# Start loads, rotation temporaries, pool waits and convolution taps of a hybrid encoder layer, rearranged

## The chip, the cores and the metric

The kernel runs on one core of one Trainium2 chip. What is measured is the time in microseconds that one execution takes on the device; the median of several runs counts. The engines are named as the profile names them: PE (TensorE, matrix products; PEld is its loading of weights), DVE (VectorE), ACT (ScalarE), POOL (GpSimd) and SP (SyncE, which here only issues transfers).

## The reference

One encoder layer is applied to two sequences with the same weights, a prompt of 512 tokens and a sample of 256, width 1024, in 32-bit floats. An attention group and a convolution group work beside each other on the same normed input:

```python
def mixer(h, ...):
    proj = h @ w_in
    cq, ckv, kr, conv_a, conv_g = jnp.split(proj, cut, axis=-1)
    q = (rms_norm(cq, q_norm_g) @ w_uq).reshape(B, S, N_HEADS, QK_NOPE + QK_ROPE)
    kv = (rms_norm(ckv, kv_norm_g) @ w_ukv).reshape(B, S, N_HEADS, QK_NOPE + V_HEAD)
    q_rope, k_rope = apply_rope(q_rope, cos, sin), apply_rope(kr, cos, sin)
    attn = block_attention(qf, kf, v)            # 8 heads, softmax over all tokens
    u = conv_a * jax.nn.sigmoid(conv_g)
    u = depthwise_conv(u, dw_w) + dw_b           # 31 taps, 512 channels, centred
    u = jax.nn.silu(layer_norm(u, conv_ln_g, conv_ln_b))
    merged = jnp.concatenate([rms_norm(attn, attn_out_g), rms_norm(u, conv_out_g)], axis=-1)
    return merged @ w_out

x = x + mixer(rms_norm(x, norm1_g), ...)
x = x + swiglu(rms_norm(x, norm2_g), w_gate, w_up, w_down)   # inner width 2816
return rms_norm(x, final_g)
```

Here `qf` and `kf` are the two parts of each head, 64 numbers without and 32 with rotation, put together; one rotated key part serves all heads.

## The kernel before, in words

Every large product is done in three: an operand is split by `split` into a high part, rounded by ACT (`L107`, with a scale `L110`), and the rest, which DVE subtracts (`L108`), and PE multiplies high by high, high by low and low by high. All products come from `mm` (`L293`). The 768 tokens are 6 blocks of 128; blocks 0 to 3 are the prompt (`s` = 0), 4 and 5 the sample.

The stages follow each other:

- *Convolution's projection.* Four blocks of channels `i`, each over eight slabs `k` of the transposed input `xT`. The slabs come through the load ring `stg`, four buffers with the tag "st", and are split into `hT` with the norm's gain `g1` as the scale. The norm's factor per token comes later: token rows `xr` (two buffers for six rows) are squared and summed by ACT, `build_rb` turns the sums into diagonal matrices `dg` (DVE) and multiplies these with ones on PE (`prb`), which spreads the factors over all partitions (`rb`). `glu(i)` then makes the convolution's input `u`.
- *Latent projections*, `tm_mm` and `tm_tr`, for query and key/value.
- *Query stage*, `q_up`, `v_up`, `k_up`, `kr_up`: heads are unfolded, `rope` rotates a part of each. `q_up` ends with ACT's copy of the block (`L470`) and a rotation of four DVE operations (`L375` to `L378`), whose temporaries `rc` and `rs` come from the pool `cTp`.
- *Attention*, 12 units. A unit transposes queries into `ptq`, splits them into `qh` and `ql`, makes the scores `pss`, takes the maxima `ngmx` (`L711`) and goes on to exponentials and values. Between the units stand the convolution's layer norms (`conv_ln`, which transposes `acc` into `pcl`), its activation, and parts of the output projection, whose results `out_add` adds to `xall` (`L815`). `LN0` is the unit after which the prompt's norm stands.
- *Output projection, SwiGLU feed-forward, final norm.* The feed-forward is by far the longest stage.

The depthwise convolution has no stage of its own. It is 240 instructions on DVE, one for each tap and block of channels (`conv_taps`, `L250`, 120 of 512 columns for the prompt and 120 of 256 for the sample), which are spread over the stages: each `mm` adds its own estimated time, multiplied by the stage's `RATE`, to what is due, and taps are issued until that is paid (`tap_some`). `tap_all` issues what is left ahead of a norm.

The written order isn't the order of execution: a scheduler with costs of its own places the instructions of each engine. `tc.keep_in_program_order` holds an instruction in the order in which it is written; `mm` uses it where `pin` is set.

Memory is taken from pools that are closed and whose place goes to others. With `reuse="pool"`, the default, the first tile of a new pool waits until all that lay in its place is through; with `reuse="tile"` each tile waits only for the tiles that lay where it lies. Ahead of the attention `wkvp`, `tb`, `cTp` and `psA` (the PSUM of all stages so far) are closed and six pools opened.

Of the kernel before, what the change touches and what calls it, by code (L numbers as in the profile page):

```python
# [11 lines left out]
F32 = mybir.dt.float32  # L12
# [5 lines left out]
PSUM = bass.MemoryType.PSUM  # L18

D = 1024  # L20
S0, S1 = 512, 256
T = S0 + S1
NB = T // 128
H, DN, DR, DV = 8, 64, 32, 64
# [11 lines left out]
C_G1, C_QG, C_KG, C_DW, C_DB, C_LG, C_LB, C_OG, C_COS, C_SIN = 0, 8, 11, 13, 137, 141, 145, 149, 157, 253  # L36
# [1 line left out]

RATE = {"A": 0.6, "B": 1.4, "C": 0.6, "D": 1.0, "S": 1.0, "F": 1.2}
SAMPLE_RATE = 0.2

TAPW = 4

LN0 = 4


@with_exitstack
def tile_hybrid_layer(  # L50
# [15 lines left out]
    nc = tc.nc  # L66
    ACT, DVE, POOL, PE = nc.scalar, nc.vector, nc.gpsimd, nc.tensor

    def pool(name, bufs=1, side="left", space=None, reuse="pool"):
        if space is None:  # L70
            cm = tc.tile_pool(name=name, bufs=bufs, side=side, reuse_waits=reuse)
        else:
            cm = tc.tile_pool(name=name, bufs=bufs, space=space, side=side, reuse_waits=reuse)
        es = ExitStack()
        p = es.enter_context(cm)
        return p, es.close
# [3 lines left out]
    stg = ctx.enter_context(tc.tile_pool(name="stg", bufs=4))  # L80
# [6 lines left out]
    def nm(s):  # L87
        uid[0] += 1
        return f"{s}_{uid[0]}"
# [15 lines left out]
    def split(dst_hi, dst_lo, src, scale=None):  # L105
        if scale is None:
            ACT.copy(dst_hi, src)  # L107
            DVE.tensor_sub(dst_lo, src, dst_hi.bitcast(F32))  # L108
        else:
            ACT.activation(dst_hi, src, AF.Copy, scale=scale)  # L110
            DVE.scalar_tensor_tensor(dst_lo, src, scale, dst_hi.bitcast(F32), ALU.mult, ALU.subtract)
# [18 lines left out]
    mhalf = cpool.tile([128, 8], F32, name="mhalf")  # L130
    DVE.memset(mhalf, -0.5)
    g1 = cpool.tile([128, 8], F32, name="g1")
    nc.gpsimd.dma_start(g1, cst[:, C_G1 : C_G1 + 8])
    c = cpool.tile([128, C_N], F32, name="c")
    r1 = cpool.tile([128, NB], F32, name="r1")
    r1sq = cpool.tile([128, NB], F32, name="r1sq")
# [14 lines left out]
    SEQ = ((0, S0), (S0, S1))  # L151
# [20 lines left out]
    cTp, cT_close = pool("cTp")  # L172
# [26 lines left out]
    def conv_chunk(i, j):  # L199
        return wsplit(wab, wconv[i, j], 1024)  # L200

    ss = small.tile([128, NB], F32, tag="ss", name="ss")
    xr = [xrp.tile([128, D], F32, tag="xr", name=nm("xr"), bufs=2) for _ in range(NB)]
# [3 lines left out]
    for k in range(8):  # L207
        if k == 4:
            wc[0, 1] = conv_chunk(0, 1)
        if k < 4:  # L210
            ks = slice(k * 256, (k + 1) * 256)
            t = stg.tile([128, 1024], F32, tag="st", name=nm("st"))
            nc.sync.dma_start(t[:, :256], wconv[0, 0][:, ks])
            split(w0[0][:, ks], w0[1][:, ks], t[:, :256])
        t = stg.tile([128, 1024], F32, tag="st", name=nm("st"))
        (nc.scalar if k == 0 else nc.sync).dma_start(t[:, :T], xT[:, k, :])
        if k == 2:
            nc.sync.dma_start(c, cst)
        for s, (o, n) in enumerate(SEQ):
            split(hT[s][0][:, k, :], hT[s][1][:, k, :], t[:, o : o + n], g1[:, k : k + 1])  # L220

    wc[1, 0] = conv_chunk(1, 0)
    for b in range(NB):
        nc.sync.dma_start(xr[b], xtok[b * 128 : (b + 1) * 128, :])
        ACT.activation(xr[b], xr[b], AF.Square, scale=1.0 / 32.0, accum_out=ss[:, b : b + 1])
        if b == 2:
            wc[1, 1] = conv_chunk(1, 1)
# [50 lines left out]
    def tap_all(s):  # L278
        while True:
            nxt = next_tap(s)  # L280
            if nxt is None:
                return
            nxt[1]()
# [8 lines left out]
    def mm(out, lhsT, rhs, start, stop):  # L292
        pinned(PE.matmul(out, lhsT, rhs, start=start, stop=stop))  # L293
        n = rhs.shape[-1]
        tap_some(n / 2400 * (4 if rhs.dtype == F32 else 1))

    pcs = {}
    pace["rate"] = RATE["A"]

# [19 lines left out]
    for i in range(4):  # L319
        pp = [psA.tile([128, 512], F32, tag="p", name=nm("pc")) for _ in range(3)]  # L320
        ps = [[pp[0], pp[2][:, :256]], [pp[1], pp[2][:, 256:]]]
        for k in range(8):
# [10 lines left out]
            for ag in range(2):  # L333
                o = (k % 4) * 256 + ag * 128
# [10 lines left out]

    pace["rate"] = RATE["B"]

# [17 lines left out]
    def rope(dst, src, b, n, tp):  # L365

        cs = c[:, None, C_COS + b * 16 : C_COS + (b + 1) * 16].to_broadcast([128, 2 * n, 16])
        sn = c[:, None, C_SIN + b * 16 : C_SIN + (b + 1) * 16].to_broadcast([128, 2 * n, 16])
        tcs = tp.tile([128, n, 2, 16], F32, tag=f"rc{n}", name=nm("rc"), bufs=2)
        tsn = tp.tile([128, n, 2, 16], F32, tag=f"rs{n}", name=nm("rs"), bufs=2)  # L370
        s4 = src.rearrange("p n (two f) -> p n two f", two=2)
        d4 = dst.rearrange("p n (two f) -> p n two f", two=2)
        cs4 = cs.rearrange("p (n two) f -> p n two f", two=2)
        sn4 = sn.rearrange("p (n two) f -> p n two f", two=2)
        DVE.tensor_mul(tcs, s4, cs4)  # L375
        DVE.tensor_mul(tsn, s4, sn4)
        DVE.tensor_sub(d4[:, :, 0, :], tcs[:, :, 0, :], tsn[:, :, 1, :])
        DVE.tensor_add(d4[:, :, 1, :], tcs[:, :, 1, :], tsn[:, :, 0, :])  # L378
# [3 lines left out]
    def loc(b):  # L382

        s = b // 4
        return s, slice((b % 4) * 128, (b % 4 + 1) * 128)
# [44 lines left out]
    for b in range(NB):  # L430
# [6 lines left out]
        if b >= 1:  # L437
            tm_tr(b - 1)
    pace["rate"] = RATE["C"]

# [18 lines left out]
    def q_up(b):  # L459
        s, bs = loc(b)  # L460
        pp = [psA.tile([128, 512], F32, tag="p", name=nm("pqu")) for _ in range(2)]
        for kk in range(3):
            for x, w in ((0, 0), (0, 1), (1, 0)):
                for n in range(2):
                    mm(
                        pp[n][:, :384], cq[s][x][:, kk, bs], wq[kk][w][:, n * 384 : (n + 1) * 384],
                        start=(kk == 0 and x == 0 and w == 0), stop=(kk == 2 and x == 1),
                    )
        for n in range(2):
            ACT.activation(qt[b][:, n * 384 : (n + 1) * 384], pp[n][:, :384], AF.Copy, scale=fq[:, b : b + 1])  # L470
        qr = qt[b].rearrange("p (h d) -> p h d", h=H)[:, :, DN:]
        rope(qr, qr, b, H, cTp)

    def v_up(b):
        s, bs = loc(b)
# [57 lines left out]

    pace["rate"] = RATE["D"]

    atp, at_close = pool("atp")
    tmp, tmp_close = pool("tmp")
    dp, dp_close = pool("dp")
    xp, xp_close = pool("xp", side="right")
    psD, psD_close = pool("psD", space=PSUM)  # L540
    psX, psX_close = pool("psX", space=PSUM, side="right")
    TAGS = {
        "s": [(psD, "s", 1), (psX, "sx", 2), (psX, "sx", 2)],
        "t": [(psD, "t", 1), (psX, "tx", 1)],
# [12 lines left out]
    rc = cpool.tile([128, NB], F32, name="rc")  # L557
# [216 lines left out]
    def load_x(b):  # L774
        x1[b] = xall[:, b * D : (b + 1) * D]
        nc.sync.dma_start(x1[b], xtok[b * 128 : (b + 1) * 128, :])
# [51 lines left out]
    for i in range(len(units) + 1):  # L828
        unit_step(i)
        if i == LN0:  # L830
            tap_all(0)
# [4 lines left out]
            pin[0] = False  # L836
        elif i == LN0 + 1:
            conv_ln(2)
            conv_ln(3)
        elif i == LN0 + 2:  # L840
            for k in range(4):
                conv_act1(0, k)
                conv_act2(0, k)
            for b in range(NB):
                load_x(b)
        elif i == LN0 + 4:
            attn_norm(4)
            attn_norm(5)
            conv_split(0)
        elif i == LN0 + 7:  # L850
            wc0 = conv_w(0)
# [500 lines left out]
    for b in range(3):  # L1352
        p = bank("hd")
# [97 lines left out]
```

## Time and profile before

| | us |
|---|---|
| median of three runs | 847.96 |
| lowest and highest of them | 845.97, 850.9 |
| time of the profiled execution | 845.79 |
| its span in the trace | 844.0 |

| stretch of the trace (us) | what runs there | PE busy | DVE busy | ACT busy |
|---|---|---|---|---|
| 0 to 36.35 | first slabs, up to `prb` | 28.10 | 17.99 | 25.39 |
| 36.35 to 126.00 | convolution's and latent projections | 89.65 | 84.81 | 30.66 |
| 126.00 to 173.77 | query stage | 39.65 | 46.20 | 35.86 |
| 173.77 to 257.87 | attention | 82.02 | 72.74 | 70.73 |
| 257.87 to 302.04 | end of the attention, norms, output projection | 39.66 | 36.80 | 20.28 |
| 302.04 to 844.00 | feed-forward and final norm | 531.06 | 456.27 | 251.44 |

How to read it: the times are those of one execution, and an engine is busy while an instruction of it runs; waiting isn't busy. In a row of the profile such as `L250 DVE SCALAR_TENSOR_TENSOR acc<-u,c,acc` stand the line of the kernel, the engine, the operation, and its output and inputs by the kernel's names; `L107`, `L108`, `L110` and `L293` are lines of helpers, so that one goes by the names. A bracket at a row's end tells how long the engine had been idle ahead of it and what ended that. The granted clock is given as a share of full speed.

### The profile page before, as it was taken

To read this page: it belongs to the slowest core of one execution; us is meant where nothing else is said; L and a number is where in the kernel's file an instruction comes from. 1 tells how busy PE (TensorE), PEld (TensorE's weight loads), DVE (VectorE), ACT (ScalarE), POOL (GpSimd) and SP (SyncE) were. 2 spreads that over 40 slices of the span, in tenths; PEclk is the share of its full clock that TensorE was granted. 3 is DMA by queue.
4 is the path that set the end of the run, shared out by engine and by line. 5 is a ranking of instruction groups with operands and counts; after the bars stand their busy time and mean duration, and the time that the engine had idled before them with its cause. 6 is when DMAs were issued, how large, how long until landed. Compare 5 with 4: busy or idle time off the path is not lost.

```text
span 844.0 us, 12490 instructions
## 1 busy us (share of the span) xinstructions
PE 810.1 (96%) x4381; PEld 722.9 (86%) x4381; DVE 714.8 (85%) x1310; ACT 434.4 (51%) x886; POOL 87.9 (10%) x113
## 2 busy tenths in 40 slices
PE   6999999879999899999999999999999999999996
PEld 5888998866766678799999999999999988888775
DVE  4699989989898855898999988898988669989993
ACT  6623337958895254784333343433334346455753
POOL 1000341001010201100000000000000000004743
PEclk9999999989999989999999999999999999999999
DMA  8812102300001231368554333444344699963344
GB/s 304 293 54 76 45 1 76 151 1 1 1 1 51 75 101 75 114 203 287 191 196 151 122 127 130 147 144 147 126 151 139 218 306 321 312 205 123 103 138 149
DMA packets 49662, 117.18 MB, mean 139 GB/s; under 512 B 5056, under 2 KB 18368, under 8 KB 49600
## 3 DMA queue, kind: packets, MB, share of 16 engines
q1 hardware_dynamic: 49424, 116.00, 40.9%
q8 instruction: 34, 0.56, 0.3%
q10 hardware_dynamic: 144, 0.39, 0.1%
q14 instruction: 28, 0.23, 0.1%
q0 software_dynamic: 32, 0.00, 0.0%
HBM read 93.96 MB, written 22.41 MB: 138 GB/s over the span
## 4 chain that ended last, share of the span: by engine, by line
PE 54%; DVE 4%; issue 3%; DMA 1%; POOL 1%; ACT 1%; POOLq 0%; ACTq 0%; DVEq 0%
PE bank L293 53%; DVE wr L108 1%; DMA sr<-wdn 1%; DVE sr L1308 1%; DVE ra L108 1%; DVE xall L1214 0%; DVE sa L108 0%; DVE xall L1227 0%; PE bank L982 0%; POOL nmv L969 0%; POOL fmv L1241 0%; POOL fmr L1242 0%; DVE vt L1218 0%; POOL nmr L971 0%; ACT vt L1226 0%
## 5 line engine op out<-in xcount | busy, mean ns | idle before, releaser
L293 PE MATMUL bank<-ra,wr 128*128 128x384 f32 x1056 | 186.6, 335 | 0.0
L293 PEld LDWEIGHTS bank<-ra,wr 128*128 128x128 f32 x1056 | 183.4, 188 | 0.0
L293 PE MATMUL bank<-sa,wr 128*128 128x384 f32 x780 | 139.2, 335 | 0.0
L293 PE MATMUL bank<-wr,wr 128*128 128x512 f32 x594 | 135.1, 389 | 1.3 <-DVE wr L108 1.3
L293 PEld LDWEIGHTS bank<-sa,wr 128*128 128x128 f32 x780 | 135.5, 188 | 0.0
L250 DVE SCALAR_TENSOR_TENSOR acc<-u,c,acc 128x512 f32<-128x512 f32 (+1 forms) x240 | 132.9, 610 | 0.1
L293 PEld LDWEIGHTS bank<-wr,wr 128*128 128x128 f32 x594 | 111.4, 188 | 24.8 <-DVE wr L108 1.7
L107 ACT CAST wr<-vt 128x512 fp32r<-128x512 f32 x88 | 54.6, 620 | 97.7 <-PE bank L293 92.6
L107 ACT CAST wr<-sr 128x512 fp32r<-128x512 f32 x106 | 64.7, 616 | 61.3 <-PE bank L293 60.0
L108 DVE TENSOR_TENSOR wr<-sr,wr 128x512 fp32r<-128x512 f32 x106 | 71.9, 683 | 14.7 <-ACT wr L107 14.7
L1236 POOL TENSOR_SCALAR fme<-fms 128x1 f32<-128x1 f32 x6 | 33.9, 5644 | 418.3 <-ACT vt L1226 418.0
L293 PE MATMUL pc<-ra,sa 128*128 128x256 f32 (+1 forms) x288 | 54.4, 350 | 8.2 <-ACT ra L110 8.2
L108 DVE TENSOR_TENSOR wr<-vt,wr 128x512 fp32r<-128x512 f32 x88 | 60.1, 685 | 0.0
L293 PEld LDWEIGHTS pc<-ra,sa 128*128 128x128 f32 x288 | 45.8, 195 | 15.8 <-ACT ra L110 8.6
L107 ACT CAST wr<-ra 128x384 fp32r<-128x384 f32 x51 | 26.0, 512 | 33.1 <-PE bank L293 21.2
L293 PE MATMUL pss<-ra,qh 96*128 96x512 f32 (+1 forms) x96 | 30.4, 397 | 6.2 <-ACT qh L107 5.3
L108 DVE TENSOR_TENSOR wr<-ra,wr 128x384 fp32r<-128x384 f32 x51 | 28.1, 551 | 8.5 <-ACT wr L107 8.3
L293 PE MATMUL bank<-wr,ra 128*128 128x512 f32 x144 | 34.2, 394 | 0.0
L293 PE MATMUL pq<-sa,ra 128*128 128x384 f32 x108 | 33.8, 342 | 0.0
L711 DVE TENSOR_REDUCE ngmx<-pss 128x1 f32<-128x512 f32 (+1 forms) x40 | 27.0, 685 | 6.2 <-PE pss L293 6.0
L293 PEld LDWEIGHTS bank<-wr,ra 128*128 128x128 f32 x144 | 26.7, 188 | 5.6
L293 PE MATMUL bank<-sa,ra 128*128 128x512 f32 x114 | 30.3, 419 | 0.1
(224 smaller groups left out, 1340.5 us busy)
## 6 DMA issues: line engine op xcount, KB each, us to landing
sr<-wgu SPq DMA_DIRECT2D x52, 512.0 KB, 3.9
sr<-wdn SPq DMA_DIRECT2D x34, 512.0 KB, 4.6
sumd<-xall SPq DMA_DIRECT2D x44, 192.0 KB, 1.9
ra<-sumd SPq DMA_DIRECT2D x44, 192.0 KB, 5.0
actd<-xall SPq DMA_DIRECT2D x11, 384.0 KB, 2.3
xall<-actd SPq DMA_DIRECT2D x11, 384.0 KB, 2.9
st<-wconv SPq DMA_DIRECT2D x7, 512.0 KB, 6.1
xr<-xtok SPq DMA_DIRECT2D x6, 512.0 KB, 6.7
```

The lines of the kernel that those rows point to most:

```text
L107: ACT.copy(dst_hi, src)
L108: DVE.tensor_sub(dst_lo, src, dst_hi.bitcast(F32))
L250: yield n / 512, lambda j=j: DVE.scalar_tensor_tensor(a, us[:, j : j + n], w(j), a, ALU.mult, ALU.add)
L293: pinned(PE.matmul(out, lhsT, rhs, start=start, stop=stop))
L711: DVE.tensor_reduce(mx, ps.rearrange("p (j n) -> p j n", j=m), AX.X, ALU.max, negate=True)
L1236: POOL.tensor_scalar(fme[b], fms[:, 2 * b + 1 : 2 * b + 2], 1.0, EPS, ALU.mult, ALU.add)
L1308: DVE.tensor_add(w, tw[f], w)
```

## The change

- `RATE["C"]`, which sets how many taps are issued in the query stage, goes from 0.6 to 0.45, and `LN0` from 4 to 5: the prompt's norm, and what is counted from it, comes one unit later.
- The gain `g1` is loaded by ACT's queue and not by POOL's. The first slab comes in two pieces, prompt and sample, each a transfer of its own.
- The loads of `c` and of the token rows are held in program order, in which they stand behind slab 2 and behind all slabs.
- The query's rotation takes its temporaries from a buffer of the load ring. `k`'s rotation, whose temporaries lie in `tb`, stays as it was.
- Five of the attention's six pools wait tile by tile.

```diff
-RATE = {"A": 0.6, "B": 1.4, "C": 0.6, "D": 1.0, "S": 1.0, "F": 1.2}
+RATE = {"A": 0.6, "B": 1.4, "C": 0.45, "D": 1.0, "S": 1.0, "F": 1.2}
...
-LN0 = 4
+LN0 = 5
...
-    nc.gpsimd.dma_start(g1, cst[:, C_G1 : C_G1 + 8])
+    nc.scalar.dma_start(g1, cst[:, C_G1 : C_G1 + 8])
...
-        (nc.scalar if k == 0 else nc.sync).dma_start(t[:, :T], xT[:, k, :])
+        if k == 0:
+            for o, n in SEQ:
+                nc.scalar.dma_start(t[:, o : o + n], xT[:, k, o : o + n])
+        else:
+            nc.sync.dma_start(t[:, :T], xT[:, k, :])
         if k == 2:
-            nc.sync.dma_start(c, cst)
+            tc.keep_in_program_order(nc.sync.dma_start(c, cst))
...
-        nc.sync.dma_start(xr[b], xtok[b * 128 : (b + 1) * 128, :])
+        tc.keep_in_program_order(nc.sync.dma_start(xr[b], xtok[b * 128 : (b + 1) * 128, :]))
...
-        tcs = tp.tile([128, n, 2, 16], F32, tag=f"rc{n}", name=nm("rc"), bufs=2)
-        tsn = tp.tile([128, n, 2, 16], F32, tag=f"rs{n}", name=nm("rs"), bufs=2)
+        if tp is None:
+            tmp_ = stg.tile([128, 1024], F32, tag="st", name=nm("st"))
+            tcs, tsn = [
+                tmp_[:, i * n * 32 : (i + 1) * n * 32].rearrange("p (n two f) -> p n two f", two=2, f=16)
+                for i in range(2)
+            ]
...
-        rope(qr, qr, b, H, cTp)
+        rope(qr, qr, b, H, None)
...
-    atp, at_close = pool("atp")
-    tmp, tmp_close = pool("tmp")
-    dp, dp_close = pool("dp")
+    atp, at_close = pool("atp", reuse="tile")
+    tmp, tmp_close = pool("tmp", reuse="tile")
+    dp, dp_close = pool("dp", reuse="tile")
     xp, xp_close = pool("xp", side="right")
-    psD, psD_close = pool("psD", space=PSUM)
-    psX, psX_close = pool("psX", space=PSUM, side="right")
+    psD, psD_close = pool("psD", space=PSUM, reuse="tile")
+    psX, psX_close = pool("psX", space=PSUM, side="right", reuse="tile")
```

The edits move instructions on all engines. At three places the order before and now is shown; the numbers behind a name tell tiles of one name apart, and lines behind the edit count up to 11 more than before.

First, SP's queue at the start, from the transfer of `c` on. `st` is a buffer of the load ring, and a row has its source. Before:

```order
L218 DMA c<-cst 128x349
L224 DMA xr_145<-xtok 128x1024
L224 DMA xr_146<-xtok 128x1024
L213 DMA st_171<-wconv 128x256
L216 DMA st_175<-xT 128x768
L213 DMA st_182<-wconv 128x256
L216 DMA st_186<-xT 128x768
L224 DMA xr_147<-xtok 128x1024
L102 DMA st_192<-wconv 128x1024
L216 DMA st_196<-xT 128x768
```

Now, from the last slab but one on:

```order
L220 DMA st_209<-xT 128x768
L220 DMA st_215<-xT 128x768
L102 DMA st_221<-wconv 128x1024
L228 DMA xr_145<-xtok 128x1024
L228 DMA xr_146<-xtok 128x1024
L102 DMA st_231<-wconv 128x1024
L228 DMA xr_147<-xtok 128x1024
L228 DMA xr_148<-xtok 128x1024
L102 DMA st_380<-wconv 128x1024
L228 DMA xr_149<-xtok 128x1024
L228 DMA xr_150<-xtok 128x1024
```

Three token rows stood ahead of slab 4; now all six stand behind slab 7, with weights between the pairs. On PE the products that need them, `prb`, stood like this before, as the 142nd instruction and after:

```order
L239 MATMUL prb_401<-dg_403,ones 128x128
L239 MATMUL prb_401<-dg_406,ones 128x128
L239 MATMUL prb_401<-dg_409,ones 128x128
L293 MATMUL pc_340<-ra_69,sa_3_71 128x512
L293 MATMUL pc_342<-ra_69,sa_3_71 128x256
L239 MATMUL prb_401<-dg_412,ones 128x128
L239 MATMUL prb_402<-dg_415,ones 128x128
L239 MATMUL prb_402<-dg_418,ones 128x128
```

Now they stand in one piece, the first of them as the 156th instruction:

```order
L297 MATMUL pc_341<-ra_69,sa_3_71 128x512
L243 MATMUL prb_402<-dg_404,ones 128x128
L243 MATMUL prb_402<-dg_407,ones 128x128
L243 MATMUL prb_402<-dg_410,ones 128x128
L243 MATMUL prb_402<-dg_413,ones 128x128
L243 MATMUL prb_403<-dg_416,ones 128x128
L243 MATMUL prb_403<-dg_419,ones 128x128
L297 MATMUL pc_343<-ra_69,sa_3_71 128x256
```

Thirteen more of the projection's matmuls stand ahead of the first `prb`.

Second, DVE at the end of the query stage: the last rotation (of which `sa` is the rotated block), the taps beside it, and the first splits and maxima of the attention. Before:

```order
L250 SCALAR_TENSOR_TENSOR acc_117<-u_125,c,acc_117 128x256
L375 TENSOR_TENSOR rc_1744<-sa_171_1423,c 128x256
L376 TENSOR_TENSOR rs_1745<-sa_171_1423,c 128x256
L250 SCALAR_TENSOR_TENSOR acc_115<-u_123,c,acc_115 128x512
L377 TENSOR_TENSOR sa_171_1423<-rc_1744,rs_1745 128x8x16
L378 TENSOR_TENSOR sa_171_1423<-rc_1744,rs_1745 128x8x16
L250 SCALAR_TENSOR_TENSOR acc_118<-u_126,c,acc_118 128x256
L250 SCALAR_TENSOR_TENSOR acc_119<-u_127,c,acc_119 128x256
L108 TENSOR_TENSOR ql_1791<-ptq_1785,qh_1790 96x512
L108 TENSOR_TENSOR ql_1804<-ptq_1798,qh_1803 96x512
L250 SCALAR_TENSOR_TENSOR acc_117<-u_125,c,acc_117 128x256
L711 TENSOR_REDUCE ngmx<-pss_1807 128x2
```

Now:

```order
L254 SCALAR_TENSOR_TENSOR acc_114<-u_122,c,acc_114 128x512
L386 TENSOR_TENSOR st_1735<-sa_171_1423,c 128x256
L387 TENSOR_TENSOR st_1735<-sa_171_1423,c 128x256
L254 SCALAR_TENSOR_TENSOR acc_115<-u_123,c,acc_115 128x512
L388 TENSOR_TENSOR sa_171_1423<-st_1735 128x8x16
L389 TENSOR_TENSOR sa_171_1423<-st_1735 128x8x16
L108 TENSOR_TENSOR ql_1781<-ptq_1775,qh_1780 96x512
L108 TENSOR_TENSOR ql_1794<-ptq_1788,qh_1793 96x512
L254 SCALAR_TENSOR_TENSOR acc_114<-u_122,c,acc_114 128x512
L722 TENSOR_REDUCE ngmx<-pss_1797 128x2
```

The two `ql` stand behind the last rotation as before; the three taps of 256 columns around it are gone, and taps of 512 columns are still there afterwards.

Third, DVE ahead of the sample's norm, whose statistics are `BN_STATS`. Before, from one addition to `xall` on:

```order
L815 SCALAR_TENSOR_TENSOR xall<-pe_2969,rc,xall 128x512
L250 SCALAR_TENSOR_TENSOR acc_116<-u_124,c,acc_116 128x256
L250 SCALAR_TENSOR_TENSOR acc_117<-u_125,c,acc_117 128x256
L250 SCALAR_TENSOR_TENSOR acc_118<-u_126,c,acc_118 128x256
L250 SCALAR_TENSOR_TENSOR acc_119<-u_127,c,acc_119 128x256
L815 SCALAR_TENSOR_TENSOR xall<-pe_2992,rc,xall 128x512
L573 BN_STATS bst_3011<-pcl_3006 128x6
```

Now, without the first six of the taps that follow the addition `xall<-pe_2958`:

```order
L254 SCALAR_TENSOR_TENSOR acc_116<-u_124,c,acc_116 128x256
L254 SCALAR_TENSOR_TENSOR acc_117<-u_125,c,acc_117 128x256
L254 SCALAR_TENSOR_TENSOR acc_118<-u_126,c,acc_118 128x256
L254 SCALAR_TENSOR_TENSOR acc_119<-u_127,c,acc_119 128x256
L826 SCALAR_TENSOR_TENSOR xall<-pe_2987,rc,xall 128x512
L584 BN_STATS bst_3006<-pcl_3001 128x6
```

Ten taps stand between the two additions, where there were four.

More of the change, by code (lines that the diff above doesn't have):

```diff
@@ L368, in rope @@
         sn = c[:, None, C_SIN + b * 16 : C_SIN + (b + 1) * 16].to_broadcast([128, 2 * n, 16])
-        tcs = tp.tile([128, n, 2, 16], F32, tag=f"rc{n}", name=nm("rc"), bufs=2)
-        tsn = tp.tile([128, n, 2, 16], F32, tag=f"rs{n}", name=nm("rs"), bufs=2)
+        if tp is None:
[4 more added lines that the diff above has]
+            ]
+        else:
+            tcs = tp.tile([128, n, 2, 16], F32, tag=f"rc{n}", name=nm("rc"), bufs=2)
+            tsn = tp.tile([128, n, 2, 16], F32, tag=f"rs{n}", name=nm("rs"), bufs=2)
         s4 = src.rearrange("p n (two f) -> p n two f", two=2)
```

## Prediction

> **What bounds the kernel now.** I read a table by stage first, then who TensorE (PE) waits for, then the timeline at the places that the change touches. In the stage table a row has the stage, its length, and for PE, weight loads, VectorE (DVE), ScalarE (ACT) and GpSimd the busy microseconds and instructions, then the granted clock.
>
> ```profile
> 126.00:167.38 41.38, 38.57 (x213) 34.77 (x212) 39.81 (x77) 35.23 (x78) 3.77 (x4) 1.00 0.33 115
> 167.38:173.77 6.39, 1.08 (x8) 0.83 (x8) 6.39 (x16) 0.63 (x2) 0.00 (x0) 0.80 0.00 1
> ...
> 181.00:257.87 76.87, 75.52 (x449) 51.95 (x447) 67.53 (x139) 67.31 (x164) 8.51 (x18) 1.00 0.00 1
> 257.87:290.50 32.63, 30.32 (x151) 20.80 (x151) 31.31 (x67) 12.40 (x27) 3.83 (x8) 1.00 0.25 81
> 290.50:302.04 11.54, 9.34 (x51) 7.63 (x50) 5.49 (x14) 7.88 (x20) 1.96 (x6) 0.95 0.00 0
> ...
> 307.70:844.00 536.30, 525.40 (x2769) 488.56 (x2767) 453.02 (x804) 247.16 (x471) 47.23 (x30) 1.00 0.52 173
> ```
>
> After 307.70 PE is busy 525.40 of 536.30 us, and the order of that part is unchanged: it moves as a block with the moment at which it begins, so everything is decided before. From 126 to 290 the bound is DVE: 39.81 of 41.38, all of 6.39 while PE stands, 67.53 of 76.87 with ACT at 67.31 beside it, and 31.31 of 32.63. PE's two longest waits in total (sum, times, longest):
>
> ```profile
> PE pc L293 <- ACT ra L110: 8.2, 2, 6.0
> PE pss L293 <- ACT qh L107: 5.3, 1, 5.3
> ```
>
> The change aims at these two. Neither ends at something that runs alone: what has to be found is who is late next.
>
> **Part 1, the loads at the start.** Token rows go behind the slabs, the norm's gain comes by ACT's queue, the first slab in two pieces.
>
> ```profile
> 6.01 10.84 PE L293 MATMUL pc<-ra,sa 128*128 128x512 f32 x48 [6.01 <-ACT ra L110]
> 19.08 17.43 PE L293 MATMUL pc<-ra,sa 128*128 128x512 f32 x96 [2.23 <-ACT ra L110]
> 20.24 1.39 SPq L102 DMA_DIRECT2D st<-wconv  x2
> 30.02 1.06 ACT L225 ACTIVATE xr<-xr 128x1024 f32<-128x1024 f32 x1
> 30.99 0.18 ACT L225 ACTIVATION_READ_ACCUMULATOR xr<-xr 128x1 f32 x1
> 32.94 0.68 DVE L238 TENSOR_SCALAR dg<-ident,r 128x128 f32<-128x128 f32 x3
> 36.35 0.83 PE L239 MATMUL prb<-dg,ones 128*128 128x128 f32 x6
> 37.96 8.37 PE L293 MATMUL pc<-ra,sa 128*128 128x512 f32 x46
> ```
>
> Unhindered, one matmul here takes 8.37 / 46 = 0.182 us. The first 48 took 10.84 instead of 8.74, and then PE stood 2.23: 4.3 us of late slabs. That is the most that slabs can bring, and 0 the least. I take 3.0: three token rows of 512 KB no longer stand ahead of slab 4, for which PE stood, but the ring of four buffers, which also holds issues back, is as it was.
>
> So PE arrives at prb 3.0 us sooner. But prb now stands 13 matmuls further on, and needs the last token row. Old time of that place, with prb behind it and 11 of the 13 still to come: 37.96 + 11 x 0.182 = 39.96. New arrival: 36.35 + 13 x 0.182 - 3.0 = 35.7. The chain of the rows: the slab transfer that SP issued at 20.24 waits for DVE's work on slab 4, and the token rows now follow right behind it, so the first is issued at about 20.24 - 3.0 + 0.3 = 17.5. There are two buffers for six rows: three rounds of a landing time L and a Square (30.02 to 31.17, 1.15), and one more Square for the pair's second row. L is bounded by rows of the transfers (last number: us from issue to landing), first a transfer alone:
>
> ```profile
> st<-wtm SPq DMA_DIRECT2D x1, 480.0 KB, 3.4
> ```
>
> Then the next one, behind it, and two token rows in today's full queue:
>
> ```profile
> st<-wtm SPq DMA_DIRECT2D x1, 480.0 KB, 4.3
> ...
> xr<-xtok SPq DMA_DIRECT2D x2, 512.0 KB, 7.0
> ```
>
> These are 3.4, 4.3 and 7.0. In the new order one or two others are in flight, so I take 4.3. The last Square ends at 17.5 + 3 x (4.3 + 1.15) + 1.15 = 35.0. From there to the end of the first dg it is 2.0 (31.17 to 33.2), then the other five dg at 0.23 and the last matmuls, 1.5: prb ends at 38.5. PE stands some 2 us in front of it, and of the 3.0 there remain 39.96 - 38.5 = **1.5 us**. Ends: L = 3.4 gives 35.8, before PE's own 35.7 + 0.83, so 3.4 gained; L = 7.0 gives 46.6, so 6.7 lost. The moved gain and the split slab (PE starts at 6.01 at the earliest slab) lie ahead of prb and are priced at nothing: the chain of the rows hides them, and without it they would be part of the 3.4. DVE's first taps start as late as before; its idle time below covers that.
>
> **Part 2, the query stage and the start of attention.**
>
> ```profile
> DVE cq L108 <- ACT cq L107: 3.8, 3, 1.6
> ...
> 158.39 0.42 DVE L375 TENSOR_TENSOR rc<-sa,c 128x256 f32<-128x256 f32 x1 [0.57 <-ACT sa L470]
> 164.26 3.07 ACT L470 ACTIVATE sa<-pqu,fq 128x384 f32<-128x384 f32 x6
> 172.75 0.28 DVE L378 TENSOR_TENSOR sa<-rc,rs 128x128 f32<-128x128 f32 x1
> 173.14 1.07 ACT L107 CAST qh<-ptq 96x512 fp32r<-96x512 f32 x2 [5.81 <-DVE sa L378]
> 173.77 1.65 PE L293 MATMUL pss<-ra,qh 96*128 96x256 f32 x6 [5.31 <-ACT qh L107]
> 173.85 1.28 DVE L108 TENSOR_TENSOR ql<-ptq,qh 96x512 fp32r<-96x512 f32 x2
> 176.31 0.69 DVE L711 TENSOR_REDUCE ngmx<-pss 128x2 f32<-128x512 f32 x1 [0.78 <-PE pss L293]
> 177.16 0.69 DVE L711 TENSOR_REDUCE ngmx<-pss 128x2 f32<-128x512 f32 x1 [0.16 <-PE pss L293]
> 178.63 0.69 DVE L108 TENSOR_TENSOR ql<-ptq,qh 96x512 fp32r<-96x512 f32 x1 [0.77 <-ACT qh L107]
> ```
>
> Today qh is released by the last rotation (172.75), by way of the pools. With waits by tile, and the temporaries in the ring, qh can go when ACT is through with L470 at 167.3. But a score needs ql too; ql is DVE's, and in the new DVE order it still stands behind the last rotation. DVE is not let off there: from the rotation that begins at 158.39 to ql, both orders hold five rotations and 13 taps of 512; only three taps of 256 are gone. The price of a tap:
>
> ```profile
> 116.58 6.04 DVE L250 SCALAR_TENSOR_TENSOR acc<-u,c,acc 128x512 f32<-128x512 f32 x9
> 260.51 5.23 DVE L250 SCALAR_TENSOR_TENSOR acc<-u,c,acc 128x256 f32<-128x256 f32 x13
> ```
>
> 0.66 us and 0.40 us. So ql comes 3 x 0.40 = **1.2 us** sooner on top of part 1, and PE's 5.31 mostly become a wait for DVE's ql of some 4 us. (Ahead of that rotation DVE is tied to PE by its waits, cq's 3.8 and 158.39's 0.57, so the five taps of 512 that the new order has fewer by then turn into idle time. The ring costs the rotations nothing: a slot's last readers are four tiles back on DVE itself.) What the waits by tile do buy: the scores' qh parts run ahead of ql, and the first maxima no longer wait. 0.78 + 0.16 + 0.77 = **1.7 us** of DVE's idle time go (ends 0 and 1.7; PE's whole 5.31 is the first rival).
>
> **Part 3, what is given back.** The taps left over must still run. From ql to the end of the last maximum at 257.87, the new order has five taps of 512 more and one of 256 less: 5 x 0.66 - 0.40 = 2.9 us of DVE work, in a stretch where DVE idles 76.87 - 67.53 = 9.3. Ends 0 (all of it fills idle time) and 2.9 (none does); neither row is nearer, so the middle, **1.5 lost**. From there to the last tap it is 49 taps instead of 43; ten instead of four stand in one piece ahead of the norm that PE waits for.
>
> ```profile
> 269.22 0.75 DVE L815 SCALAR_TENSOR_TENSOR xall<-pe,rc,xall 128x512 f32<-128x512 f32 x1 [1.32 <-issue]
> ...
> 288.89 1.86 PE L570 MATMUL pcl<-ident,acc 128*128 128x128 f32 x8 [0.83 <-DVE acc L250]
> ```
>
> 6 x 0.40 = 2.4, less the 1.32 of idle time, which they fill: **1.1 lost** (ends 0 and 2.4). PE's 0.83 grows to about 3. The norm one unit later and the x rows that SP now issues ahead of the output weights cost nothing: the weights have some 85 us from the last rotation, which frees their slots, to their splits at the end of the attention.
>
> **Sum:** -1.5 - 1.2 - 1.7 + 1.5 + 1.1 = -1.8 us. The profiled execution took 845.79 (span 844.0 and 1.8 around it), which gives 844.0. It lies 2.2 under the median 847.96 of the runs; against the median the forecast is **846.2**. Its own range, with part 1 between L = 3.4 and 5 and the other ends, is 842 to 850.
>
> [...] In two stretches the granted clock was half:
>
> ```profile
> 173.77:178.00 4.23, 4.23 (x20) 4.20 (x21) 3.11 (x6) 0.44 (x1) 0.00 (x0) 0.50 0.00 0
> 302.04:307.70 5.66, 5.66 (x14) 4.44 (x15) 3.25 (x7) 4.28 (x7) 1.59 (x2) 0.50 0.44 134
> ```
>
> PE, working through both, lost at most half their length there, 2.1 and 2.8 us. The first follows PE's pause of 5.31; the second follows 290.50 to 302.04, where PE was busy 9.34 of 11.54. I leave both in the sum: a pause of about 4 us stays at the first, and the wait ahead of the second grows. [...]
>
> **The rivals.**
> - *The start of attention really opens* (0.27). PE's 5.31 go whole, and part 1 brings 3.4: 847.96 - 8.7 = 839.3. For it: DVE idles 9.3 + 1.3 us between 181 and 290.5, room for it. Against it: ql behind the rotations, and the same 120 and 120 taps to finish before PE's norm.
> - *The token rows are late* (0.12). With L = 7.0 PE loses 6.7 at prb: 847.96 + 6.7 - 0.3 = 854.4. Part 1 turns to a loss from L = 4.8, the whole is worse by half a per cent from about 6.3. Against it: 7.0 belongs to a queue with more transfers ahead.
> - *The clock stays up* (0.09), with the rest as forecast: 846.2 - 4.9 = 841.3. For it: both waits move in time against whatever sets those stretches. Against it: both remain.
>
> **How the numbers follow.** The likeliest has 0.52, and 846.2 is its time. Half a per cent, 4.2 us, is about what a measurement of this kernel can tell from no change; its three runs alone span 845.97 to 850.9. Faster (under 843.7): the first rival, two thirds of the third, a tenth of the likeliest, 0.38. Slower (over 852.2): three quarters of the second and a little of the likeliest, 0.11. Within: the remaining 0.51. The range holds the likeliest, most of the first and third, and the lighter half of the second: 837 to 853.
>
> **What would show it.** Right: the 2.23 at pc gone, a new wait of prb for DVE's dg of 1 to 3 us; qh several us ahead of ql, and PE waiting for ql; pcl waiting about 3 us for the taps; token rows landing 4 to 5 us after issue. Wrong: no wait at prb, ql within 3 us of the last L470, or DVE's idle time from ql to the last tap well under 10 us, which is the fast case; landings over 6 us, the slow one.

## The result and the profile after

The changed kernel is slower: a median of 859.39 us (858.79 to 861.73, four runs) against 848.83 (845.97 to 850.9, four runs), a ratio of 1.0136 with a 95% interval of 1.009 to 1.0182. (The ratios, here and below, are estimated from all runs and can differ a little from the quotient of the two medians.) Of all runs two are left out as disturbed, 4555.62 and 856.57 us, both of the kernel with only the token rows let go. The profiled execution took 859.5 with a span of 857.7, 13.7 more than the span before; the profile of before was a short one of its kernel, so some 3 us of these 13.7 are not in the medians.

The stage table of after, cut at the same places of the work as that of before: up to the first `prb`, to the first latent projection, to the end of the last `q_up`, to the first `ptp`, to the last score, to the sample's norm `pcl`, to the first matmul of the feed-forward, to the end (length, then PE, PEld, DVE, ACT, POOL busy, granted clock, DMA share, GB/s).

```profile
0.00:44.20 44.20, 30.86 (x157) 25.28 (x157) 16.18 (x30) 23.48 (x38) 3.10 (x24) 0.96 0.76 250
44.20:87.34 43.14, 43.14 (x240) 37.82 (x240) 41.22 (x65) 15.07 (x22) 0.00 (x0) 0.96 0.30 89
87.34:173.82 86.48, 84.47 (x520) 80.95 (x519) 80.79 (x157) 51.56 (x126) 19.84 (x24) 1.00 0.15 50
173.82:184.88 11.06, 5.77 (x31) 4.82 (x29) 10.03 (x22) 2.96 (x8) 0.00 (x0) 0.69 0.53 160
184.88:268.81 83.93, 80.17 (x453) 55.43 (x454) 70.06 (x143) 68.24 (x168) 8.82 (x18) 0.94 0.00 1
268.81:303.01 34.20, 30.04 (x152) 20.79 (x150) 33.30 (x72) 13.49 (x29) 3.83 (x8) 1.00 0.23 77
303.01:316.02 13.01, 11.69 (x57) 9.37 (x57) 7.20 (x17) 7.48 (x19) 1.97 (x6) 0.87 0.00 0
316.02:857.70 541.68, 529.88 (x2783) 492.26 (x2782) 457.31 (x810) 252.45 (x479) 51.44 (x32) 0.99 0.53 172
```

And the attention's row of before at these cuts:

```profile
179.12:257.07 77.95, 76.48 (x457) 53.08 (x458) 68.34 (x140) 68.39 (x169) 8.51 (x18) 1.00 0.00 1
```

| place | before | after | later by |
|---|---|---|---|
| first product of DVE with `rb` | 38.66 | 47.23 | 8.57 |
| first latent projection | 80.09 | 87.34 | 7.25 |
| first `ptp` | 179.12 | 184.88 | 5.76 |
| last score | 257.07 | 268.81 | 11.74 |
| sample's norm, `pcl` | 288.89 | 303.01 | 14.12 |
| feed-forward | 302.04 | 316.02 | 13.98 |

So 7.25 are lost ahead of the latent projections, 1.5 come back in the query stage, 6.0 are lost in the attention and 2.4 behind it; the feed-forward moves as a block, as forecast. In three kernels below with the same loads and the same place of `prb` the first latent projection comes only 4.8 to 5.4 late (84.89, 85.07, 85.47), so this execution lies at the long end.

Counted on DVE, up to the end of the last tap, the loss is 14.12 (304.05 against 289.93), and its parts are these. The first product with `rb` comes 8.57 later. From there to the first `ql` DVE takes 2.35 less (132.84 against 135.19): ten taps fewer, but two splits of weights more, which it did ahead of `rb` before. From `ql` to the last maximum it takes 5.95 more (90.05 against 84.10), of which 2.40 is work (75.17 against 72.77) and 3.55 is idle time. From there to the last tap it takes 1.95 more, for five more taps of 256 columns. DVE's longest wait in the attention, for PE's scores, before and after:

```profile
DVE ngmx L711 <- PE pss L293: 5.1, 11, 1.6
DVE ngmx L722 <- PE pss L297: 9.7, 10, 2.3
```

PE's waits (sum, times, longest):

```profile
PE pc L297 <- ACT ra L110: 7.3, 3, 6.0
PE prb L243 <- DVE dg L242: 6.0, 1, 6.0
PE pss L297 <- DVE ql L108: 4.6, 1, 4.6
PE pcl L581 <- DVE acc L254: 3.2, 1, 3.2
```

The 2.2 at `pc` are 1.3 now (7.3 holds the 6.0 of the start), and `qh` is hardly waited for. New are 6.0 at `prb`, 4.6 at `ql`, 3.2 at `pcl`: three waits that the prediction named, the first three times as long as forecast. The chain of the token rows, from the timeline:

```profile
20.27 0.90 SPq L228 DMA_DIRECT2D xr<-xtok  x2
27.91 1.60 SPq L228 DMA_DIRECT2D xr<-xtok  x2
32.69 3.12 SPq L228 DMA_DIRECT2D xr<-xtok  x2
40.96 1.06 ACT L229 ACTIVATE xr<-xr 128x1024 f32<-128x1024 f32 x1 [2.88 <-DMA xr<-xtok]
42.14 0.17 DVE L236 TENSOR_SCALAR v<-ss 128x6 f32<-128x6 f32 x1 [4.33 <-ACT xr L229]
42.40 1.35 POOL L237 TENSOR_TENSOR r<-v,mhalf 128x6 f32<-128x6 f32 x1 [40.10 <-DVE v L236]
44.20 2.93 PE L243 MATMUL prb<-dg,ones 128*128 128x128 f32 x12 [6.02 <-DVE dg L242]
47.23 0.68 DVE L308 TENSOR_TENSOR t<-pc,rb 128x512 f32<-128x512 f32 x1
```

Three rounds of two rows, issued at 20.27, 27.91 and 32.69 and on; the last Square ends at 42.1. Then the power on POOL, the diagonals, `prb`, and only at 47.23 has DVE its first product with `rb`. DVE waits 4.33 there, and 5.01 shortly before.

### The profile page after: what moved, and what is told of

Read it like the earlier page. It is cut to its first block, busy times and chain, and to the rows that moved or that the text cites. A ratio compares the mean times of both kernels' runs of the same rounds, so it can differ in the third digit from the quotient of the medians.

```text
span 857.7 us, 12481 instructions
## 1 busy us (share of the span) xinstructions
PE 816.0 (95%) x4381; PEld 726.7 (85%) x4381; DVE 716.1 (83%) x1310; ACT 434.7 (51%) x886; POOL 89.0 (10%) x112
## 4 chain that ended last, share of the span: by engine, by line
PE 73%; DVE 11%; ACT 6%; DMA 5%; issue 4%; POOL 1%; ACTq 0%; SPq 0%; POOLq 0%; DVEq 0%
PE bank L297 51%; PE pc L297 5%; PE pss L297 3%; PE pq L297 3%; PE po L297 3%; DVE acc L254 2%; PE pt L297 2%; DVE wr L108 2%; DMA xr<-xtok 2%; PE ptp L742 2%; ACT ra L468 1%; DMA sr<-wdn 1%; DMA st<-wconv 1%; ACT sa L725 1%; DVE xall L1225 1%
## 5 line engine op out<-in xcount | busy, mean ns | idle before, releaser
L1247 POOL TENSOR_SCALAR fme<-fms 128x1 f32<-128x1 f32 x6 | 36.5, 6080 | 420.8 <-ACT vt L1237 420.6
L725 ACT ACTIVATE sa<-pss,ngmx 128x512 f32<-128x512 f32 (+1 forms) x48 | 29.4, 622 | 1.8 <-DVE ngmx L722 1.8
```

The costliest lines, as they stand in the source:

```text
L725: ACT.activation(P[:, js], ps[:, js], AF.Exp, bias=ngmx[:, b0 + b, h : h + 1], accum_out=asum[:, b0 + b, h : h + 1],)
L1247: POOL.tensor_scalar(fme[b], fms[:, 2 * b + 1 : 2 * b + 2], 1.0, EPS, ALU.mult, ALU.add)
```

## The experiments

Four kernels first ask which part of the change costs the time, four more by which way, four more whether the reasons lead to a faster kernel. The expectations of the first runs name two theories, A and B, and explain them. Those of the later runs name three. W: PE's own waits are the loss. D: DVE, which bounds the kernel from the start of the taps to the last norm, follows the moment at which it gets `rb`. C: PE's clock falls where PE has little to stream, and that costs time in the attention.

**The loads as before, the rest changed.**

```diff
-    nc.scalar.dma_start(g1, ...)                          # changed kernel
+    nc.gpsimd.dma_start(g1, ...)
...
-        tc.keep_in_program_order(nc.sync.dma_start(xr[b], ...))
+        nc.sync.dma_start(xr[b], ...)
```

(and slab 0 in one piece, `c` not held in order)

> The changed kernel with the loads at the start as before (gain by POOL's queue, first slab in one piece, transfer of c and token rows not held in order); the rest of the change stays. In the changed kernel PE is 7.25 us late at the first latent projection, loses 6.0 more in the attention and 2.2 at the last norm, and gains 1.6 in the query stage. Theory A (the token rows alone are late, the attention's loss belongs to the norm that stands one unit later): the 7.25 go and the rest stays, 859.4 - 7.3 = 852, with a stretch of half clock still in the attention. Theory B (the late start pushes taps into the attention, and that is its loss): 7.25, 6.0 and 2.2 go, 859.4 - 15.5 = 844, no half clock in the attention.

Measured: 848.57 (841.09 to 852.05, ten runs) against 848.02, ratio 1.0001, 0.9962 to 1.0041. All of the loss comes by the loads; what else was changed is worth nothing in sum that these runs can tell (the interval is 0.4% to either side). In its trace the first `ql` is at 172.58 (before 173.85), the last maximum ends at 257.88 (257.95), the last tap at 290.97 (289.93), and the feed-forward begins at 302.70 (302.04). Theory A of the expectation, by which the norm's new place costs the attention its 6.0, falls. B is right that all comes from the loads, but its 844 lies some 4 too low: the time is that of before. Nor is the attention free of half clock, as B had it: a stretch from 172.2 to 182.4 reaches 5.0 us into it.

**The loads alone, in the kernel before.**

> The kernel before with the four edits of the loads only. Both theories: PE waits some 6 us at prb. Theory A: 848.8 + 7.3 = 856, and the attention as long as before (77.95 us from the first ptp to the last score). Theory B: 848.8 + 7.3 + 6 + 2 = 864 at most, the attention longer by several us, with a stretch of half clock, since its taps come late here too.

Measured: 858.23 (854.95 to 862.48, four runs), ratio 1.0117, 1.0054 to 1.0179. The loss is here again, without pools, rotations, `RATE` and `LN0`, and it is 10 us, not the 7 of the start. The attention from the first `ptp` to the last score takes 87.93 instead of 77.95, as B said and A did not; the time lies between A's 856 and B's 864. The first latent projection starts at 84.89, 4.8 late: PE's wait at `prb` was 3.28 here, and 4.1 and 5.1 in two kernels below whose start is that of the changed kernel, so the 6.0 of the profile after lies at the long end.

**Only the token rows let go of the order**; gain, slab 0 and `c` as changed.

> The changed kernel with only the token rows let go of the program order; gain, first slab and c stay as changed. If the place of the rows is the whole of the start's loss: no wait at prb over 1 us, first latent projection at 80 or earlier, and the time within 1.5 us of the kernel with all loads as before. Rival (the split slab or the gain by ACT's queue costs as well): PE still 2 us or more later than before at the first latent projection.

Measured: 848.6 (842.0 to 853.57, eight runs), ratio 0.9985, 0.9946 to 1.0025; no wait at `prb`, first latent projection at 80.64. The place of the token rows is the cause; the other three edits of the loads cost nothing that can be measured. Its trace and that of the first experiment give something more. Their attentions hold the same instructions in the same order, and DVE and ACT work the same time in them:

```profile
177.38:257.15 79.77, 77.33 (x452) 54.02 (x453) 68.39 (x140) 68.08 (x167) 9.16 (x18) 0.97 0.00 1
```

This row is the kernel with all loads as before; the next the one with only the rows let go:

```profile
178.45:263.07 84.62, 82.29 (x452) 56.78 (x453) 68.51 (x140) 68.35 (x167) 9.17 (x18) 0.91 0.00 1
```

4.85 us longer, with a granted clock of 0.91 instead of 0.97. What is missing from the full clock is PE's time: 0.09 x 84.62 = 7.6 against 0.03 x 79.77 = 2.4, a difference of 5.2. So the clock alone makes some 5 us of the attention, with the same work, in one pair of executions. In the second kernel, as in the changed one, a stretch of half clock 10.2 us long lies in the middle of the attention; in the first none does.

**Three buffers for the token rows** (`bufs=2` to `bufs=3` for `xr`).

> The changed kernel with three buffers for the token rows instead of two, so two rounds instead of three. If the chain of transfer and Square through two buffers sets the end (theory A and B both): a round of about 7 us goes, less what three rows in flight land later, so the last Square ends at about 38 instead of 42.1, PE's wait at prb falls from 6.0 to about 2, and the time to 855. Rival (the bytes in the queue set it, not the buffers): landings grow to 8 us and more, the last Square still ends at about 42, 859.

Measured: 858.53 (857.81 to 861.03, four runs), ratio 1.0123, 1.0071 to 1.0174. The chain behaved as both theories said:

```profile
18.93 1.39 SPq L228 DMA_DIRECT2D xr<-xtok  x3
26.55 2.89 SPq L228 DMA_DIRECT2D xr<-xtok  x3
```

Two rounds, the last Square done at 36.7 instead of 42.1, PE's wait 3.0, the first latent projection at 83.15, 4.2 sooner than after. But the time is only 0.9 less, within what the runs scatter. Of the 4.2, 3.1 are left at the first `ql` (176.96 against 180.07) and 1.6 at the last tap (302.49 against 304.05). The expected 855 was wrong: shortening PE's wait doesn't shorten the whole by as much. Nor does an earlier `rb` by itself, so the run also speaks against the simple form of D, by which everything moves with `rb`. DVE had `rb` at 41.11, 6.1 sooner than in the profile after, and 3.1 and 3.8 sooner than in two profiles below with the loads of the changed kernel (44.19 and 44.94); only for the sample's part it waited until 43.50. From there to `ql` it took 3.0 more than after, of which 1.1 was idle time and the rest one split and one tap more, and from `ql` to the last maximum 1.5 more, all of it idle time.

**`prb` two slabs later.**

```diff
-            if i == 1 and k == 4:
+            if i == 1 and k == 6:
                 build_rb()
```

> The changed kernel with build_rb and glu(0) two slabs later in the convolution's second block (k == 6 instead of 4), so that PE has some 11 matmuls more to do before the first prb. The token rows are as late as in the changed kernel. Theory W (PE's wait of 6.0 us at prb is the loss): the wait falls to about 3 or less, the time by as much, to 856 or below, and the first latent projection starts at 84 or earlier. Theory D (DVE is the bound: it can't begin its 240 taps before rb is there, 8.6 us later than before, and nothing gives that back): DVE's first product with rb stays at about 47, ql and the last tap come as late as in the changed kernel or later, and the time stays at 858 to 861 although PE waits less.

```profile
PE prb L243 <- DVE dg L242: 2.4, 2, 1.6
44.63 0.69 DVE L308 TENSOR_TENSOR t<-pc,rb 128x512 f32<-128x512 f32 x1
```

Measured: 857.38 (856.32 to 859.8, four runs), ratio 1.0101, 1.0048 to 1.0154. PE's wait falls by 3.6, and the first latent projection starts at 83.53, as W said; the time falls by 2.0 and lies between the two forecasts. DVE had its `rb` at 44.63 here, 2.6 sooner than in the profile after, though its place was to be as late: this start varies by that much between executions (44.19 and 44.94 in the next two profiles, where `prb` stands as in the changed kernel). Read by itself the run doesn't tell W from D.

**Twelve taps of the prompt left out**, which separates them better: PE has the same work, DVE 7.9 us less. (The result is no longer that of the layer.)

```diff
-        for j in range(1, KW):
+        for j in range(1, KW - 3 * (1 - s)):
```

> The changed kernel without the last three of the 31 taps on the prompt: 12 DVE instructions of 512 columns fewer, 12 x 0.66 = 7.9 us of DVE work left out ahead of the attention. Theory D: DVE's late start is made good by these 7.9 us: time 859.4 - 8 = 851, and more if the stretch of half clock in the attention goes too. Theory W: PE still waits 6.0 at prb and its own work is the same; the time falls by at most the 3.2 that PE waits for the last taps, 856 or above.

```profile
PE prb L243 <- DVE dg L242: 5.1, 1, 5.1
...
182.93:262.01 79.08, 76.65 (x452) 53.43 (x453) 68.39 (x140) 68.08 (x167) 9.16 (x18) 0.98 0.00 1
```

Measured: 847.62 (845.22 to 853.84, ten runs), ratio 0.9985, 0.9956 to 1.0014: 11.8 less than the changed kernel, back at the time before, with PE's wait of 5.1 at `prb` still there. W (856 or above) falls: the time follows DVE's work, as D has it, and work taken from DVE makes the loss good. That the late start is the whole loss isn't shown by this: the kernel before was not run with the same taps left out, and the fall is 3.9 more than the 7.9. The attention is 4.85 shorter than after's 83.93, at a clock of 0.98 instead of 0.94; only 1.7 of that is DVE's work (68.39 against 70.06).

**Wide small products.** `prc` sums squares by a matrix of ones, two columns wide. In the profile after, eight of them stand on either side of a wait of 1.60; the fifth row is the stretch behind it:

```profile
235.86 0.95 PE L297 MATMUL prc<-ones,th 128*128 128x2 f32 x8
238.40 0.80 PE L297 MATMUL pss<-ra,qh 96*128 96x512 f32 x2 [1.60 <-ACT sa L725]
239.00 0.63 PE L297 MATMUL pss<-ra,ql 96*128 96x512 f32 x1
239.43 1.70 PE L297 MATMUL prc<-ones,th 128*128 128x2 f32 x8
...
238.92:249.16 10.24, 10.24 (x37) 7.04 (x38) 6.30 (x14) 6.67 (x17) 1.49 (x3) 0.50 0.00 0
```

The second eight take 1.70 instead of 0.95: the clock was halved from 238.9 to 249.2. The experiment computes 64 equal columns and reads one (the taps that these products pay for stay as they were).

```diff
-                pr[:, 2 * b : 2 * b + 2], th[:, b * 128 : (b + 1) * 128], ones[:, :2],
+                pr[:, 64 * b : 64 * b + 64], th[:, b * 128 : (b + 1) * 128], ones[:, :64],
```

> The changed kernel with the small products prc (row sums of squares by a matrix of ones) 64 columns wide instead of 2, of which one column is read as before. In the changed kernel PE has half clock from 238.9 to 249.2, right behind a stretch with 1.60 us of waiting and eight prc. Theory C (the clock falls where PE has too little to stream, waiting or not, and the half clock is worth some 5 us of the attention): the 64 columns keep it up, no half clock in the attention, time 859.4 - 4 = 855. Rival (the attention is bound by DVE and ACT, so PE's clock there is free, or the width doesn't move the clock): 858 to 860.

> The kernel before with prc 64 columns wide. Theory C: no half clock from 300.9 on, where eight prc stand ahead of the feed-forward; that stretch cost at most 2.8 us, and the runs with a mean clock of 0.984 lose their second stretch too: 2 to 4 us less, 844 to 846. Rival: no change, 848.

Measured on the changed kernel: 855.43 (850.85 to 859.06, ten runs), ratio to before 1.0072, 1.0042 to 1.0102, 4.0 less than without. The stretch in the attention became shorter, 6.8 instead of 10.2 us, and didn't go, so the size came out as expected and the picture only in part: 3.4 us less of half clock give at most 1.7 of the 4.0. The mean clock over its runs is 0.9825, over those of the changed kernel 0.978; 0.0045 x 857 = 3.9 us would fit. On the kernel before: 845.4 (841.24 to 851.82, twelve runs) against 849.51, ratio 0.9972, 0.9939 to 1.0005, which just fails to show a gain. The granted clock at the end of the output projection, before and with wide `prc`:

```profile
296.00:308.00 12.00, 11.11 (x45) 9.16 (x44) 6.78 (x15) 10.39 (x25) 1.59 (x2) 0.72 0.24 73
296.00:308.00 12.00, 11.17 (x52) 9.33 (x53) 7.40 (x16) 10.62 (x24) 1.41 (x2) 0.86 0.21 61
```

Half as much is lost there; the mean clock over its runs is 0.992, and 0.988 over the runs of before beside it.

**`prb` one slab earlier, in the kernel before** (`k == 4` to `k == 3`), alone and with wide `prc`.

> The kernel before with build_rb and glu(0) one slab earlier (k == 3), where the diagonals stand ready at 33.2 and PE arrived only at 36.35. Theory D (everything up to the last norm follows the moment at which DVE gets rb): DVE's first product with rb comes 2.2 us earlier, 36.5 instead of 38.66, and so does the last tap, 287.7 instead of 289.9; time 848.8 - 2.2 = 846.6. Theory W (PE's waits are what counts): there was no wait at prb, so nothing changes, 848.8.

> The kernel before with both: prc 64 columns wide, and build_rb one slab earlier. Theories C and D together: 2.2 less than the kernel with wide prc alone (ratio 0.9972 to before), so a ratio of 0.9946, 844.5. If D is wrong: 0.997.

Measured: 847.77, ratio 0.9989 (0.9964 to 1.0014), and 846.34, ratio 0.9972 (0.9951 to 0.9993), twelve runs each. In the first trace `rb` comes 1.3 sooner (37.36) and the last tap 1.2 sooner (288.75), so the shift goes through to the end of the taps, as D says; it was smaller than the forecast 2.2, and times alone don't resolve it. In the second trace PE was held up by half clock from 20.6 on, behind its wait for a slab, and `rb` came only 0.5 sooner than before (38.18): nothing was gained beyond the wide products.

**Matmuls in PE's pause ahead of `ql`**, in the changed kernel with the loads as before and wide `prc`.

```diff
+                if un == 0 and b == 0 and j == 0:
+                    for _ in range(34):
+                        pinned(PE.matmul(ps[:, js], qh[:, q_], kh, start=True, stop=True))
```

> The changed kernel with the loads as before and prc wide, and 34 idle matmuls of 256 columns on PE (their result is overwritten) in its pause of 5 us ahead of the first ql, which keep it streaming. Theory C: no stretch of half clock from 172 on (10.2 us in the kernel without them, of which PE worked through 9), the first units of the attention 2 us faster, ratio 0.994. Rival: DVE and ACT bound the attention and get nothing from the clock there, 0.997, or 1.000 if the idle matmuls push ql's scores back.

> The same with build_rb one slab earlier. Theory D: another 2.2 us less than the kernel without that, ratio 0.992, 842. If D is wrong: as the kernel without it.

Measured: 844.96 (eleven runs), ratio 0.9967, 0.9945 to 0.9989; with `prb` a slab earlier 842.63 (841.46 to 843.5, six runs), ratio 0.9937, 0.9918 to 0.9956. The second beats both kernels. The first is where the rival had it (0.997), and no better than wide products alone on the kernel before (0.9972); C's 0.994 lies just outside the interval. The two differ only in the slab of `prb`: DVE has `rb` at 36.76 instead of 38.92, and the time is 2.3 us less, where D said 2.2. Of the three pairs that differ in this alone, it is the only one whose times show it.

The pause, in the timeline of the second:

```profile
167.24 4.34 PE L717 MATMUL pss<-ra,qh 96*128 96x256 f32 x34 [0.29 <-ACT qh L107]
171.42 0.40 PE L293 MATMUL pss<-ra,qh 96*128 96x256 f32 x2
172.91 0.39 PE L293 MATMUL pss<-ra,ql 96*128 96x256 f32 x1 [1.09 <-DVE ql L108]
...
177.87 0.33 PE L742 MATMUL ptp<-ident,sa 128*128 128x128 f32 x1 [2.35 <-DVE ngmx L722]
```

The 5 us at `ql` shrink to 1.09, the scores run at full clock, and PE then waits 2.35 for the maxima; the half clock comes from 179.5 on, for 6.8 us, instead of from 172.2 for 10.2. So it moved and became shorter, and didn't go as C had it. A second thing works with it: beside the 34 matmuls the scheduler placed the taps anew, 81 instead of 73 between the first `ql` and the last maximum, and PE's wait of 2.6 at `pcl` is gone. How much of the gain is clock, how much the taps' place and how much the wide products was not separated.

## Why the prediction was wrong

**Part 1, "-1.5", is the step that failed**; measured are 7.25 lost at the first latent projection, and 10.2 in the time (the loads alone). It put the end of `prb` at 38.5; it came at 47.13. Its terms:

- *"I take 3.0" for the late slabs.* PE reached `prb` at 38.18 in the changed kernel. By the prediction's own working the old time of that place is 36.35 + 13 x 0.182 = 38.7: 0.5 was gained, and 1.2 to 1.9 in the three other kernels with the same loads and the same place of `prb`. In the trace the slabs' issues still follow the splits that free a buffer of the ring, slabs 4, 5 and 7 at 13.26, 13.68 and 18.83 (before 13.00, 13.43 and 18.09); the rows ahead of them were not what held them.
- *First token row at 17.5.* It was issued at 20.27, since the weights ahead of it waited for their buffer until 19.89. (The transfer issued at 20.24 before, which the prediction calls a slab's, is one of weights, `wconv`.)
- *L = 4.3.* The three rounds took 7.25, 5.04 and 5.40 us for their second row, 5.9 on average. The reference rows for 3.4 and 4.3 were a transfer alone and the next one behind it; here two rows and a weight tile stood in the queue together. The last Square so ended at 42.1 and not at 35.0. That the end at L = 7.0, "46.6", was nearly met is luck: L was 5.9, the first issue 2.8 late, and the way from the last Square to the end of `prb` took 5.0 and not 3.5.
- *"DVE's first taps start as late as before; its idle time below covers that."* This is the sentence that cost most. DVE could not start before `rb`, 8.57 later. From there to the first `ql` it had 6.4 us of idle time in 135 before, in waits that come again in every trace (5.5 to 8.0), and in the attention its idle time grew, so there was no cover. The prediction said itself that DVE is the bound from 126 to 290, and then priced late rows at PE's wait alone. The experiment with 12 taps fewer shows that the time follows DVE's work; that the start is the main part is read from the account above, 8.57 of 14.12.

The rival "token rows late" had the late rows right. That its price of 6.7 met the 7.25 is luck in part, by the same sums; its 854.4 is 5 too low since it stopped at `prb`. The 850 at the upper end of the prediction's own range is added up wrongly: its ends give 0.6 - 1.2 + 2.9 + 2.4 = 4.7, so 852.7 on the median, still far below what was measured.

**Part 3, "1.5 lost" in the attention, was 6.0.** The order holds 115 taps ahead of the first `ql` instead of 125, and 123 with the loads as before, although `RATE` was at 0.45 in both; with the loads alone, and `RATE` at 0.6, it holds 117. So the place of the rows, not the rate, made the scheduler move them. The prediction had counted the moved taps, 2.9 us of work, and 2.4 were measured. What it had not is that DVE would wait longer for PE there: the larger part of the 6.0 is the half clock from 238.9 to 249.2, 10.2 us and so up to 5.1 lost. The rival on the clock was looked for at the two places of before; that a new stretch might come in the attention wasn't.

**Part 2 and the rest of part 3 were right in their sum where the loads didn't disturb them.** They sum to -1.2 - 1.7 + 1.5 + 1.1 = -0.3, and the kernel with the loads as before has 1.0001, the feed-forward 0.7 later. `ql` came 1.3 sooner (of which 0.5 from the start), PE's 5.31 turned into a wait for `ql` of 5.0 (said: about 4), and from the last maximum to the last tap it took 1.1 more, as said. Between `ql` and the last maximum, though, -1.7 + 1.5 came out as 1.2 more (85.30 against 84.10), so the sum is in part luck. The first rival, that the start of the attention opens, failed as argued: `ql` stands behind the rotations.

**What stays open:** why each of the five profiles with late rows and all taps has a stretch of half clock in the attention, when of the two with rows let go one has it and one hasn't. These two run the same matmuls there, with the same two waits of some 0.4 each near it, so the order and the waits alone don't decide it. Of the five, the longest wait of PE near the stretch was 1.60 in three, 0.89 with the loads alone and 0.55 with wide products. It isn't chance of the profiled executions alone: the mean clock is 0.976 to 0.984 in the sixteen runs of the four kernels with late rows, all taps and narrow products, and 0.982 to 0.994 in the 76 runs of before beside the experiments. How much of the loss in the medians is the later start and how much the clock is therefore not separated.

## What to carry to other kernels

A transfer that is moved back is priced at the engine that starts its long work with it, not only at the engine that shows the wait: here PE waited 3 to 6 us, and the larger part of the loss was DVE's start, 5 to 9 us later, with little behind it to take it up. A landing time is taken from rows with as many transfers in flight as there will be: 4.3 came from the second of two transfers, and with two rows and a weight tile in the queue it was 5.9. Idle time of the bound engine that is made of short recurring waits covered nothing here (DVE's 6.4 us in 135 ahead of `ql`).

## What the runs showed of the hardware

PE's clock fell within long pauses and outside them. Within: at 171.2 in the pause of 5.31 us ahead of the scores in the profile before, at 40.9 in the one of 6.02 at `prb` and at 177.5 in the one of 4.58 at `ql` in the profile after. Outside: at 238.9 in the profile after, behind 3.4 us with 1.60 of waiting and eight products of two columns, and at 300.9 in the profile before, behind 3.4 us with 0.59 of waiting and twelve such products. With wider products these two stretches were shorter, 6.8 instead of 10.2 and 3.4 instead of 6.8 us, in one trace each. In the profiles before and after the stretches, each at a granted clock of 0.50, lasted 6.8 and 6.8 us (before) and 6.8, 6.8, 10.2, 3.4 and 3.4 us (after), not counting the last of each, which ends with the trace. A stretch in the attention cost about 5 us in the pair of traces with the rows let go (84.62 against 79.77), and the runs of before scatter with the clock: of 76 runs beside the experiments, those with a mean clock of 0.986 or less have a median of 850.6, those of 0.991 and above 845.2.

Not all of the scatter is clock. From its first matmul to the end of the span the feed-forward took 539.0 to 547.7 us in the fourteen traces, and the three longest have 3.9 to 8.0 us of half clock in it, the others 2.4 to 9.5. In 200 us of it, in the profile before and in the one with twelve taps fewer, PE is busy throughout at a granted clock of 1.00 and yet gets through 2% fewer matmuls (1157 and 1135):

```profile
360.00:560.00 200.00, 200.00 (x1157) 200.00 (x1158) 179.01 (x323) 85.52 (x152) 0.00 (x0) 1.00 0.51 172
362.00:562.00 200.00, 200.00 (x1135) 200.00 (x1134) 177.96 (x318) 84.12 (x149) 0.00 (x0) 1.00 0.50 168
```

What slows it is not shown. A comparison of single executions is therefore safer up to the feed-forward than over the whole span.
